# Three instead of two chunks of the memory queries with seven block products

## The chip, the cores and the metric

The kernel runs on one core of a Trainium2 chip. The metric is the device time of one launch in microseconds. TensorE (PE) multiplies; VectorE (DVE), ScalarE (ACT) and GpSimd (POOL) do the rest; SyncE (SP) issues the weight transfers.

## The reference

One decoder layer on 256 tokens of width 2048, in float32: a half-weighted SwiGLU, a mixer (gated spatial MLP beside windowed attention), cross-attention to 256 memory rows, a second half-weighted SwiGLU, and a last RMSNorm. The part around the change is the cross-attention:

```
q = (hn @ w_q).reshape(b, s, X_HEADS, X_HEAD_DIM)      # 256 x 2048 times 2048 x 2048, 4 heads of 512
kv = memn @ w_kv
scores = einsum('bshd,bmhd->bhsm', q, k) * X_HEAD_DIM ** -0.5
probs = softmax(scores)
out = einsum('bhsm,bmhd->bshd', probs, v).reshape(b, s, D_MODEL)
return out @ w_o
```

hn is RMSNorm(h) with the gain g_x, and h the residual stream.

## The kernel before, in words

**Products.** Every large matrix product is split in a high and a low part of fp32r (hi x hi, lo x hi, hi x lo), so each block product costs three matmuls of 128 x 128 weights against 512 columns. A product is cut into *units* of 1024 output columns (two blocks of 512), and a unit into 8 *chunks* of 256 rows of the weight. Over a chunk, a 2 x 2 block matrix of the activations (two token blocks, two row blocks) meets a 2 x 2 block matrix of the weights. `PRODUCTS` gives three ways to do that, one letter each: N, the plain 8 block products (24 matmuls); C, 8 block products arranged so that their sums share banks with S (24 matmuls); S, seven block products (21 matmuls). For S the activations need four more sums (`fill`, lines 219 to 238) and the weights four sums T1 to T4, which are then split in high and low parts as well (`load`, lines 328 to 359). Sums and splits are done by ScalarE (the high part, line 147) and VectorE (the low part, line 148; the sums, lines 337 to 341).

**Banks.** There are 8 PSUM banks in two pools of 4. A unit accumulates P2, Q3, Q4, Q5 in one pool (`acc`). The products that occur in S alone, P1, Q6 and Q7, take three banks of the other pool (`trp`) from the first S chunk of the unit on, until `seven_early` has read them behind the last S chunk. The pieces of side work use the same pool. `seven_late` combines the rest behind chunk 7.

**Buffers.** Raw weights have 3 buffers, their high and low parts 2 each, the sums T and their parts one each.

**Order on TensorE.** The order of TensorE is written by hand: chunk after chunk, and between them side work. `Unit.run` (line 425) calls `side_step` after every 6 matmuls; I call that a turn. A chunk of 24 matmuls has 4 turns, one of 21 has 3. Side work consists of generators; each step of one is a piece, and its `yield n` says after how many turns the next step may come. The core of it:

```
def side_step():
    now[0] += 1
    if ends[0] is not None and now[0] > ends[0]:
        return
    if not held[0] and not (tight[0] and now[0] < piece[0] + 3):
        for item in side:
            if item[0] <= now[0]:
                ...                    # one step of this item
                return
```

`tight` holds from the first S chunk of a `seven_unit` to its last: there pieces keep three turns apart. `have(pairs, i)` runs side work at once until the pair that a chunk needs exists. The order of the other engines is left to a planner, which follows the order of the program and when it takes an input to be ready.

**The stage of the change.** `KINDS_X` names the kinds of the 8 chunks of the two units `xq` (w_xq, lines 1371 to 1375); their activations are the pairs n3, made by `next_norm` (line 800) and shared by both units. Pairs 0 to 3 are made during the unit before, 4 to 7 in the first xq unit. Behind each xq unit `late_xq` puts two generators `attend_memory` (line 1296) on the list, one a head. Their steps: start (yield 1), transposes of the queries xqTp, twice (1, then 4), scores xs with softmax (5), transposes of the probabilities xpT (3), outputs xo, twice (1 each), and an empty last step. Heads 0 and 1 are attended during the second xq unit, heads 2 and 3 during the first unit of the output projection `xo` (w_xo). That is an `added_unit` (line 657) with the kinds NNNNNSNN: its S chunk takes all four `trp` banks, chunk 4 before it allows only two turns (`clear`), and chunk 5 asks for pair 7, so that all side work is done by then. Both heads' outputs are the pairs of this product, in order.

Other units: the memory keys and values (`mk`, `mv`) use `KINDS_M`, CCSCSCSC; the SwiGLU units use CCSCSCSC and SCSCSCSC.

Of the kernel before, what the change touches and what calls it, by code (L numbers as in the profile page):

```python
# [33 lines left out]
def layer_kernel(  # L34
# [528 lines left out]
    ORDER = ((0, 1, 2, 3, 4, 5, 6, 7), (0, 1, 3, 2, 4, 5, 6, 7))  # L563
    KINDS_M = "CCSCSCSC"
    KINDS_MIX = "CCCSCCSC"
    KINDS_X = "CCCSCSCC"

    KINDS_O = "NNNSNSNN"
    HALVES_O = ("NNNNNSNN", "NNNSNSNN")
# [21 lines left out]
    def seven_unit(s, kinds, w, cb, pairs, dst, late=None, beside=None, alone=(), order=range(8)):  # L591

        kinds = "".join(kinds[i] for i in order)
        u = Unit(s, kinds, alone=alone, sparse=True)
        got = {}

        def end():
            if dst is None:
                at = {(0, 0): got["p1"], (1, 1): s2(s), (0, 1): got["v"], (1, 0): got["z"]}
                seven_late(u, got, lambda tb, j: at[tb, j])  # L600
                late(at)
                return
            seven_late(u, got, dst)
            if late is not None:
                late()

        for i in range(8):
            push(
                u, i, w[order[i], cb], lambda i=i: have(pairs, order[i]),
                lambda i=i: (i == kinds.rindex("S") and seven_early(u, got), i == 7 and end()),  # L610
                beside=beside,
            )
# [674 lines left out]
    shared.clear()  # L1287
    n3, on3, rs3_ = next_norm("n3", G_X, KINDS_X)
    for cb in range(2):
# [74 lines left out]
    def late_xq(cb, at):  # L1364
        rs = rs3_()
        for j in range(2):
            for tb in range(TB):
                nc.scalar.activation(at[tb, j], at[tb, j], AF.Copy, scale=rs[:, tb:tb + 1])
            side_add(attend_memory(2 * cb + j, [at[tb, j] for tb in range(TB)]))

    for cb in range(2):
        seven_unit(
            "xq", KINDS_X, w_xq, cb, n3, None, lambda at, cb=cb: late_xq(cb, at),
            lambda i: rs3_() if i == 3 else None,
# [135 lines left out]
```

## Time and profile before

| | |
|---|---|
| median of 3 runs (lowest to highest) | 2034.7 us (2034.1 to 2034.9) |
| profiled execution, its own time | 2033.63 us |
| its span, 24271 instructions | 2031.9 us |
| TensorE busy | 2015.5 us (99%), granted clock 0.999 |
| TensorE weight loads | 1668.8 us (82%) |
| VectorE busy | 1853.6 us (91%) |
| ScalarE busy | 1313.2 us (65%) |
| first xq unit, from the span's start | 1135.06 to 1179.11 us |
| second xq unit | 1179.11 to 1235.98 us |

Times inside the profile are microseconds from the span's start. Matmuls overlap: the profile gives each some 0.39 us, while they follow each other every 0.227 us, so a busy TensorE is judged by the chain of waits, where each piece stands with the time that it adds. A row of a timeline has start, length, engine, line, operation, output and inputs, and in brackets how long the engine sat idle before it and what ended that.

### The profile page before, as it was taken

To read this page: it belongs to the slowest core of one execution; us is meant where nothing else is said; L and a number is where in the kernel's file an instruction comes from. 1 tells how busy PE (TensorE), PEld (TensorE's weight loads), DVE (VectorE), ACT (ScalarE), POOL (GpSimd) and SP (SyncE) were. 2 spreads that over 40 slices of the span, in tenths; PEclk is the share of its full clock that TensorE was granted. 3 is DMA by queue.
4 is the path that set the end of the run, shared out by engine and by line. 5 is a ranking of instruction groups with operands and counts; after the bars stand their busy time and mean duration, and the time that the engine had idled before them with its cause. 6 is when DMAs were issued, how large, how long until landed. Compare 5 with 4: busy or idle time off the path is not lost.

```text
span 2031.9 us, 24271 instructions
## 1 busy us (share of the span) xinstructions
PE 2015.5 (99%) x9203; PEld 1668.8 (82%) x9203; DVE 1853.6 (91%) x1994; ACT 1313.2 (65%) x1460; POOL 34.4 (2%) x57
## 2 busy tenths in 40 slices
PE   9999999999999999999999999999999999999998
PEld 7788888888888888888888888888888888888886
DVE  6999999999999978989879987899999999999998
ACT  7765566567665766755566666676656666676664
POOL 0000000000000010200000000000000000000000
PEclk9999999999999999999999999999999999999999
DMA  8666666666556575544675544556566656665563
GB/s 312 197 206 225 215 218 205 236 209 220 196 191 219 177 252 178 202 166 166 208 227 182 198 160 145 187 187 224 197 239 215 215 205 231 214 219 206 187 228 125
DMA packets 115333, 415.83 MB, mean 205 GB/s; under 512 B 61824, under 2 KB 63888, under 8 KB 68112
## 3 DMA queue, kind: packets, MB, share of 16 engines
q1 hardware_dynamic: 112768, 407.14, 57.6%
q0 software_dynamic: 2016, 6.30, 1.0%
q8 instruction: 72, 1.18, 0.2%
q10 hardware_dynamic: 432, 0.84, 0.1%
q14 instruction: 45, 0.37, 0.1%
HBM read 398.52 MB, written 2.10 MB: 197 GB/s over the span
## 4 chain that ended last, share of the span: by engine, by line
PE 85%; DVE 9%; issue 3%; ACT 2%; DMA 2%; SPq 0%; POOL 0%; POOLq 0%; DVEq 0%; ACTq 0%
PE f1gQ L428 12%; PE f2gQ L428 12%; PE f2dQ L428 6%; PE f1dQ L428 6%; PE f1gP L428 5%; PE f2gP L428 4%; PE xqQ L428 3%; PE f2dP L428 3%; PE f1dP L428 3%; PE woQ L428 2%; PE xoQ L428 2%; PE f2dR L428 2%; PE f1dR L428 2%; DVE f1gwl L148 2%; PE vQ L428 2%
## 5 line engine op out<-in xcount | busy, mean ns | idle before, releaser
L148 DVE TENSOR_TENSOR f1gwl<-f1gw,f1gwh 128x1536 fp32r<-128x1536 f32 (+2 forms) x94 | 181.6, 1934 | 24.5 <-ACT f1gwh L147 23.8
L147 ACT CAST f2gwh<-f2gw 128x1536 fp32r<-128x1536 f32 (+1 forms) x88 | 150.5, 1712 | 66.4 <-PE f2gQ L428 44.9
L148 DVE TENSOR_TENSOR f2gwl<-f2gw,f2gwh 128x1536 fp32r<-128x1536 f32 (+1 forms) x88 | 179.1, 2036 | 8.0 <-ACT f2gwh L147 8.0
L147 ACT CAST f1gwh<-f1gw 128x1536 fp32r<-128x1536 f32 (+2 forms) x94 | 153.1, 1629 | 45.0 <-PE f1gQ L428 19.3
L147 ACT CAST f1gth<-f1gt 128x1024 fp32r<-128x1024 f32 x76 | 79.9, 1051 | 103.1 <-DVE f1gt L337 68.7
L147 ACT CAST f2gth<-f2gt 128x1024 fp32r<-128x1024 f32 x82 | 85.4, 1050 | 64.2 <-DVE f2gt L341 34.0
L428 PE MATMUL f2gQ<-f2gwh,n4fh 128*128 128x512 f32 x317 | 123.8, 390 | 0.6 <-DVE f2gv L587 0.6
L428 PE MATMUL f2gQ<-f2gwh,n4fl 128*128 128x512 f32 x317 | 123.4, 389 | 0.0
L428 PE MATMUL f1gQ<-f1gwh,n1fl 128*128 128x512 f32 x286 | 111.4, 390 | 1.7 <-DVE n1fl L148 1.7
L428 PE MATMUL f1gQ<-f1gwh,n1fh 128*128 128x512 f32 x286 | 111.6, 390 | 0.0
L147 ACT CAST f2dwh<-f2dw 128x2048 fp32r<-128x2048 f32 (+1 forms) x44 | 77.4, 1758 | 47.5 <-PE f2dQ L428 39.5
L147 ACT CAST f1dwh<-f1dw 128x2048 fp32r<-128x2048 f32 (+1 forms) x44 | 77.3, 1757 | 43.7 <-PE f1dQ L428 42.7
L148 DVE TENSOR_TENSOR f1dwl<-f1dw,f1dwh 128x2048 fp32r<-128x2048 f32 (+1 forms) x44 | 92.0, 2092 | 12.0 <-ACT f1dwh L147 11.8
L148 DVE TENSOR_TENSOR f2dwl<-f2dw,f2dwh 128x2048 fp32r<-128x2048 f32 (+1 forms) x44 | 92.0, 2091 | 11.2 <-ACT f2dwh L147 11.1
L148 DVE TENSOR_TENSOR f2gtl<-f2gt,f2gth 128x1024 fp32r<-128x1024 f32 x82 | 99.5, 1218 | 1.0
L428 PE MATMUL f2gQ<-f2gwl,n4fh 128*128 128x512 f32 x317 | 96.7, 389 | 0.0
L148 DVE TENSOR_TENSOR f1gtl<-f1gt,f1gth 128x1024 fp32r<-128x1024 f32 x76 | 92.2, 1216 | 0.5
L428 PE MATMUL f1gQ<-f1gwl,n1fh 128*128 128x512 f32 x286 | 86.9, 389 | 0.0
L428 PEld LDWEIGHTS f2gQ<-f2gwh,n4fh 128*128 128x128 f32 x317 | 59.5, 188 | 13.8 <-DVE f2gv L587 1.6
L428 PEld LDWEIGHTS f2gQ<-f2gwh,n4fl 128*128 128x128 f32 x317 | 59.5, 188 | 12.2
L428 PEld LDWEIGHTS f2gQ<-f2gwl,n4fh 128*128 128x128 f32 x317 | 59.4, 188 | 12.3
L428 PE MATMUL f2gP<-f2gwh,n4fh 128*128 128x512 f32 x176 | 68.6, 390 | 0.0
(824 smaller groups left out, 6072.2 us busy)
## 6 DMA issues: line engine op xcount, KB each, us to landing
f2gw<-in_w_gu SPq DMA_DIRECT2D x88, 1024.0 KB, 4.9
f1gw<-in_w_gu SPq DMA_DIRECT2D x86, 1024.0 KB, 4.8
f1dw<-in_w_down SPq DMA_DIRECT2D x44, 1024.0 KB, 4.8
f2dw<-in_w_down SPq DMA_DIRECT2D x44, 1024.0 KB, 4.8
wow<-in_w_out SPq DMA_DIRECT2D x16, 1024.0 KB, 4.8
xqw<-in_w_xq SPq DMA_DIRECT2D x16, 1024.0 KB, 4.8
xow<-in_w_xo SPq DMA_DIRECT2D x16, 1024.0 KB, 4.8
qw<-in_w_in SPq DMA_DIRECT2D x8, 1024.0 KB, 4.8
```

The source lines that it names most:

```text
L147: nc.scalar.copy(hi, src)
L148: nc.vector.tensor_tensor(lo, src, hi.bitcast(F32), ALU.subtract)
L428: nc.tensor.matmul(self.banks[name], x, y, start=name not in self.begun, stop=self.left[name] == 0)
```

## The change

One string. The kinds of the 8 chunks of both xq units become CCSCSCSC: chunks 2, 4 and 6 are S, where 3 and 5 were. The pairs n3 follow (pairs 2, 4, 6 of kind S; the others of kind C), and so do the weights that `load` prepares, the span of `tight` (chunks 2 to 6 instead of 3 to 5), the place of `seven_early` (behind chunk 6 instead of 5) and the number of turns in a unit (29 instead of 30).

```diff
     ORDER = ((0, 1, 2, 3, 4, 5, 6, 7), (0, 1, 3, 2, 4, 5, 6, 7))
     KINDS_M = "CCSCSCSC"
     KINDS_MIX = "CCCSCCSC"
-    KINDS_X = "CCCSCSCC"
+    KINDS_X = "CCSCSCSC"
```

## The prediction

> **What bounds the kernel now.** I read the head of the page, then the chain of waits over the two units of memory queries and the output projection behind them, then busy times stage by stage.
>
> ```profile
> PE 2015.5 (99%) x9203; PEld 1668.8 (82%) x9203; DVE 1853.6 (91%) x1994; ACT 1313.2 (65%) x1460; POOL 34.4 (2%) x57
> ...
> 1135.06:1179.11 44.05, 44.05 (x203) 36.49 (x203) 37.09 (x43) 31.04 (x41) 1.12 (x1) 1.00 0.55 192
> 1179.11:1235.98 56.87, 56.86 (x307) 48.70 (x307) 44.80 (x54) 36.75 (x52) 0.00 (x0) 1.00 0.43 156
> ...
> 1441.00:1482.00 41.00, 41.00 (x183) 33.96 (x182) 40.42 (x38) 25.23 (x21) 0.00 (x0) 1.00 0.64 227
> ```
>
> Columns: stretch, length, then busy PE, PEld, DVE, ACT, POOL, clock, DMA share, GB/s. The first two stretches are the two xq units, the third lies in the second SwiGLU. TensorE is never idle in them, at full clock. VectorE has 7.0 us to spare in the first unit and 12.1 in the second; in the third it is busy 40.42 of 41.00 us and TensorE still loses nothing.
>
> ```profile
> 1153.27 1.36 PE xqP L428 x6
> ...
> 1158.03 0.91 PE xqP L428 x4
> ...
> 1163.47 1.36 PE xqP L428 x6
> ...
> 1190.74 2.86 PE xs L169 x24
> ...
> 1197.71 2.87 PE xs L169 x24
> ...
> 1203.33 0.44 PE xpT L1332 x4
> ```
>
> These are rows of the chain (start, length, what). A matmul costs 1.36/6 = 0.227 us. Chunk 3, of kind S, runs from 1153.27 to 1158.03 = 4.76 us (21 matmuls); chunk 4, of kind C, to 1163.47 = 5.44 us (24). What lies on the path here is TensorE's own program order, with the attention pieces (xs scores, xpT transposes, xo outputs) set between matmuls.
>
> **The change, part by part.**
>
> *TensorE.* Each unit gets S at chunks 2, 4, 6 instead of 3, 5: one more S, 3 matmuls fewer. Two units: 6 x 0.227 = **-1.36 us**, all on the path.
>
> *Weight splitting.* One more S load in each unit.
>
> ```profile
> L147 ACT CAST xqwh<-xqw x16: 1482/1906/1921, 1127.8 to 1218.8; 128x2048 fp32r<-128x2048 f32 x12, 128x1536 fp32r<-128x1536 f32 x4
> L148 DVE TENSOR_TENSOR xqwl<-xqw,xqwh x16: 1748/2284/2293, 1129.9 to 1220.7; 128x2048 fp32r<-128x2048 f32 x12, 128x1536 fp32r<-128x1536 f32 x4
> ...
> L337 DVE TENSOR_TENSOR xqt<-xqw x4: 1217/1222/1226, 1137.2 to 1199.3; 128x1024 f32<-128x1024 f32 x4
> L340 DVE TENSOR_TENSOR xqt<-xqt,xqw x4: 680/686/694, 1138.5 to 1200.5; 128x512 f32<-128x512 f32 x4
> L341 DVE TENSOR_TENSOR xqt<-xqt,xqw x4: 682/685/692, 1139.2 to 1203.5; 128x512 f32<-128x512 f32 x4
> ...
> L147 ACT CAST xqth<-xqt x8: 1037/1046/1070, 1139.5 to 1208.0; 128x1024 fp32r<-128x1024 f32 x8
> L148 DVE TENSOR_TENSOR xqtl<-xqt,xqth x8: 1212/1218/1226, 1142.0 to 1211.4; 128x1024 fp32r<-128x1024 f32 x8
> ```
>
> VectorE for S: 1.22 + 0.69 + 0.69 (sums) + 1.75 + 2 x 1.22 (splits) = 6.79 us; for C: 2.28. So +4.5 us a unit on VectorE, and 1.48 + 2 x 1.05 - 1.91 = +1.7 on ScalarE. Among the pairs of n3 made inside the first unit (4 to 7) there are two of kind S instead of one, under 1 us more. VectorE's first unit becomes 37.1 + 5.4 = 42.5 of 43.4 us, or 98%; the second 49.3 of 56.2. The third stretch above (99%, alternating C and S) shows TensorE fed at such a share, so I take **0**. Cover is VectorE's 7 us of idle time; gone, at most the excess over it would show: 0 to 2 us, from bunching early in the unit. The 16 loads of 1 MB on SP's queue keep size and order.
>
> *Where the attention pieces go.* This is counted in the code. After every 6 matmuls comes a turn (4 in C, 3 in S); a turn may issue one piece; from first to last S pieces keep 3 turns apart. Head 0 and head 1 of a unit's output are attended during the next 8 chunks. For the second xq unit before, the count puts the pieces of head 0 / head 1 at turns: transposes 2, 3 / 5, 6; xs 7 / 10; xpT 12 / 23; xo 15 and 18 / 26 and 27, which are the starts that the chain shows (xs at 1190.74 and 1197.71, xpT at 1203.33). After, with the spaced region from chunk 2 to 6: xs 7 / 10; xpT 13 / 25; xo 16 and 19 / 28 and 29 of 29. All twelve still fit, but an empty last step of head 1 falls into the next unit's first turn, and everything of heads 2 and 3 behind it (first output projection unit) comes one turn later. There chunks 0 to 3 give 16 turns and chunk 4 only two; at chunk 5 what is left is forced out at once, since S there needs all four PSUM banks.
>
> Three prices follow.
>
> (a) *Bank in chunk 2.* S takes three of the four side banks (P1, Q7, Q6) from its start to the end of chunk 6. Now head 1's xs comes 12 matmuls into that chunk, with only the bank that head 0's xs still holds. Before, S began a chunk later. The bank is free after the second exponential's sum:
>
> ```profile
> 1199.43 0.20 ACT L1320 ACTIVATION_READ_ACCUMULATOR pr<-xs,xmx 128x1 f32 x1
> ...
> 1204.43 0.20 ACT L1320 ACTIVATION_READ_ACCUMULATOR pr<-xs,xmx 128x1 f32 x1
> ...
> 1247.40 2.95 PE xs L169 x24
> ...
> 1253.37 0.20 ACT L1320 ACTIVATION_READ_ACCUMULATOR pr<-xs,xmx 128x1 f32 x1
> ```
>
> xs ends at 1193.60, 1200.58 and (chain: 1247.40 + 2.95) 1250.35: the release comes 6.0, 4.1 and 3.2 us later. The room is 18 matmuls = 4.1 us, so the stall is 0 to 1.9. Same place, same work: 6.0, less the 0.53 by which S's first split (1.75) is shorter than C's (2.28) in the queue ahead: **+1.4**. Behind it nothing runs on TensorE; VectorE gains time.
>
> (b) *Chunk 4 of the projection.* It needs head 2's first output.
>
> ```profile
> 1264.64 1.43 PE xo L169 x12
> ...
> 1267.46 1.43 PE xo L169 x12
> 1268.89 0.93 PE xoP L428 x4
> ...
> 1271.64 0.44 PE xpT L1332 x4
> ...
> 1274.85 2.87 PE xo L169 x24
> ...
> 1266.11 0.59 ACT L147 CAST xofh<-xo 128x512 fp32r<-128x512 f32 x1 [0.36 <-PE xo L169]
> ...
> 1266.73 0.69 DVE L148 TENSOR_TENSOR xofl<-xo,xofh 128x512 fp32r<-128x512 f32 x1 [0.51 <-ACT xofh L147]
> ```
>
> Now xo (1264.64) has 6 matmuls and the second xo before chunk 4 begins at 1268.89. One turn later it is the last thing ahead of chunk 4: its end to the low half is 1267.42 - 1266.07 = 1.35 us, and the chunk's second matmul reads that half. **+1.35**; ends 0.6 (high half alone) and 2.
>
> (c) *Head 3's transposes.* Now they run from 1271.64 to 1272.08, at the last allowed turn of chunk 4; after, that turn goes to head 2's closing step, and xpT is forced out with the two xo (the row of 24 at 1274.85) directly behind it.
>
> ```profile
> 1272.12 0.59 ACT L147 CAST xpTs<-xpT 128x512 fp32r<-128x512 f32 x1 [0.17 <-PE xpT L1332]
> ...
> 1272.74 0.69 DVE L148 TENSOR_TENSOR xpTs<-xpT,xpTs 128x512 fp32r<-128x512 f32 x1
> 1274.99 2.29 DVE L148 TENSOR_TENSOR xowl<-xow,xowh 128x2048 fp32r<-128x2048 f32 x1 [1.56 <-ACT xowh L147]
> 1277.19 0.68 DVE L148 TENSOR_TENSOR xofl<-xo,xofh 128x512 fp32r<-128x512 f32 x1
> ```
>
> At best the low half is there 1.34 us after the transposes (1272.08 to 1273.43). But issued at 1274.85 they would end at 1275.29 (0.44 long), while VectorE is in the 2.29 us split of chunk 6's weights and starts its next work at 1277.19; then 0.69: 1277.9. **+2.6**, ends 1.3 and 3.3 (head 0's own: 1203.77 to 1207.03).
>
> ```profile
> 1206.36 0.67 DVE L148 TENSOR_TENSOR xpTs<-xpT,xpTs 128x512 fp32r<-128x512 f32 x1
> ```
>
> Nothing on TensorE fills these waits, though chunk 5's weights are ready:
>
> ```profile
> 1315.72 0.50 PE L428 MATMUL xoQ<-xoth,xofh 128*128 128x512 f32 x1 [1.17 <-ACT n4r L266]
> ```
>
> Here one matmul waits 1.17 us for a bank, and the following ones wait with it. [...]
>
> The end of the units (P1 copied, the combinations in one chunk instead of two) I cost at nothing: VectorE's seven combinations a unit (the row below) take 4.8 us in all, against 5.4 us of chunk 7, and the memory key units already run the new order CCSCSCSC:
>
> ```profile
> L586 DVE TENSOR_TENSOR xq<-xqQ,xqz x2: 683/684/684, 1176.6 to 1233.4; 128x512 f32<-128x512 f32 x2
> ...
> 960.43:1002.85 42.42, 42.42 (x192) 35.24 (x192) 36.95 (x36) 21.30 (x19) 0.69 (x1) 1.00 0.54 198
> ```
>
> The last row's 183 matmuls are 41.5 us and one attention piece 0.8: no gap. Without cover, 0.5. Equally the 1.17 us wait above could go or double when ScalarE's order moves: 0, ends -1.2 and +1.2.
>
> **Sum**: -1.36 + 1.4 + 1.35 + 2.6 = +4.0 us. The profiled execution took 2033.63 (span 2031.9 and 1.7 around it), 1.1 below the median of the runs, 2034.7. By the median: **2038.7 us**.
>
> **Rivals.**
>
> 1. *Full gain.* Waits are hidden: the softmax clears its bank within 4.1 us (two of three rows do), and the order on ScalarE and VectorE is arranged so that the late pieces arrive in time. 2034.7 - 1.4 = 2033.3. Against it: the one-turn slip is certain by count, and (b) has no work between producer and consumer. [...]
>
> 2. *Small net loss.* Only (b) and the low end of (c): -1.36 + 1.35 + 1.3 = +1.3, so 2036.0. It decides if the low half of xpTs goes ahead of the weight split on VectorE.
>
> 3. *VectorE becomes the bound in the first unit.* At 98% a late S split of chunk 4 stalls TensorE. It decides when VectorE's backlog passes the spare 0.9 us: with 2 us of bunching and (a) to (c), +6.0, so 2040.7. Against: the SwiGLU row at 99%.
>
> **How the numbers follow.** The measurement tells 0.2% (4.07 us) from no change: 2030.6 to 2038.8. Forecast (+3 to +5) 0.45, rival 2 (0 to +3) 0.25, rival 1 (below 0) 0.12, rival 3 (above +5) 0.18. The forecast sits on the edge of the band: half of it, and rival 3, count as slower, 0.41; rivals 1 and 2 with the other half as same, 0.55; faster 0.04, for orders elsewhere that fall better. Range: from 2033.9, in rival 1, to 2041.9: the upper ends of (a), (b) and (c) give 2040.6, and 1.3 of the bunching comes to it. About 0.1 is left out on each side.
>
> **What would show it.** In the trace after: xqP and xqQ 3 matmuls fewer a unit; a wait of TensorE ahead of head 1's xs in chunk 2 of the second unit (a); a gap of about 1.3 us ahead of the projection's chunk 4 (b); xpT directly ahead of the row of 24 xo, with 1.3 to 2.6 us between (c). No gap at these places proves rival 1 right; gaps inside the first unit that end at VectorE's splits, rival 3. I would be wrong as well if the pieces do not slip by one turn, or if the later stages shift by themselves.

## The result, and the profile after

The changed kernel takes 2045.18 us in the median of 4 runs (2044.91 to 2049.38), the kernel before 2034.4 us (2032.45 to 2034.9): 1.0058 of the time before, 95% interval 1.0045 to 1.0071, so 10.8 us slower. The prediction was 2038.7 us with a range to 2041.9: the direction was right, the size was not.

The head of the page, and the two xq units, in the same cut as before (chunk 0 of the first unit to chunk 0 of the projection):

```profile
PE 2019.4 (99%) x9197; PEld 1671.9 (82%) x9197; DVE 1862.5 (91%) x2006; ACT 1316.6 (64%) x1464; POOL 33.9 (2%) x57
```

```profile
1134.58:1178.43 43.85, 43.68 (x200) 35.86 (x200) 40.87 (x50) 31.85 (x42) 0.69 (x1) 1.00 0.57 205
1178.43:1234.64 56.21, 56.14 (x304) 48.12 (x304) 45.62 (x53) 38.10 (x49) 0.00 (x0) 1.00 0.43 150
```

TensorE has 6 matmuls fewer (9197 for 9203) and is busy 3.9 us longer. The two units together take 100.06 us instead of 100.92: 0.86 us of the 1.36 arrive. The loss comes behind them. The list of TensorE's own waits (total, times, longest) begins before with these two, which the changed kernel has as well; from 1130 to 1293 us it has none:

```profile
PE f1gQ L428 <- DVE n1fl L148: 1.7, 1, 1.7
PE xoQ L428 <- ACT n4r L266: 1.2, 1, 1.2
```

After, it has these:

```profile
PE xoQ L428 <- DVE xqv L587: 2.9, 1, 2.9
PE xo L169 <- DVE xpTs L148: 2.1, 1, 2.1
...
PE xoP L428 <- DVE xofl L148: 1.1, 1, 1.1
PE xo L169 <- ACT xpTs L147: 0.8, 1, 0.8
PE xoP L428 <- ACT xofh L147: 0.7, 1, 0.7
...
PE xqP L428 <- DVE xqwl L148: 0.2, 1, 0.2
```

All but the last stand in the first unit of the output projection, in chunk 0 (xqv: line 587 still reads the bank that the matmul needs), ahead of chunk 4 (xofh, xofl: the high and low half of head 2's output) and around head 3's xo (xpTs: its transposed probabilities). Two of them are followed by something that no row of before has. The chain first (start, length, what), then busy times by stretch (granted clock third from the end), the last row from before:

```profile
1238.88 2.93 PE xoQ L428 x6
...
1283.51 5.28 PE xo L169 x23
1288.79 1.88 PE xoP L428 x6
```

```profile
1236.00:1238.00 2.00, 0.03 (x1) 0.00 (x0) 2.00 (x3) 0.28 (x1) 0.00 (x0) 1.00 0.00 0
1238.00:1240.00 2.00, 1.11 (x3) 0.93 (x4) 2.00 (x5) 1.26 (x2) 0.00 (x0) 0.63 0.79 233
1240.00:1242.00 2.00, 2.00 (x7) 1.57 (x5) 1.28 (x5) 1.61 (x4) 0.00 (x0) 0.52 0.72 299
...
1284.00:1286.00 2.00, 2.00 (x11) 2.00 (x11) 0.00 (x0) 0.00 (x0) 0.00 (x0) 0.50 0.66 266
1286.00:1288.00 2.00, 2.00 (x12) 2.00 (x11) 0.69 (x1) 0.59 (x1) 0.00 (x0) 0.50 0.52 217
```

```profile
1236.00:1293.00 57.00, 57.00 (x309) 49.01 (x308) 45.83 (x57) 37.45 (x56) 0.00 (x0) 1.00 0.39 137
```

Six matmuls take 2.93 us instead of 1.36, 23 xo take 5.28 instead of 2.75 (0.12 each): TensorE runs at about half clock (a granted clock of 0.50 to 0.52 where a row lies wholly behind a wait) behind each of the two long waits. The mean clock fell from 0.999 to 0.996.

The sum, from chunk 0 of the first xq unit to chunk 5 of the projection: before 1277.72 - 1135.06 = 142.66 us, after 1288.79 - 1134.58 = 154.21, +11.55. The terms: -1.36 (matmuls), +0.5 (chunk 4 of the first xq unit), +2.9 and +1.6 (chunk 0's wait, and the half clock behind it), +1.7 (ahead of chunk 4), +2.9 and +3.0 (head 3's xo, and the half clock on them and on the six matmuls behind). That is +11.2; 0.3 are spread.

Theory A for the experiments: the pieces come later, TensorE waits for them in order, and its clock halves behind the longer waits. Theory B: the third S chunk's work on VectorE makes everything late, wherever the pieces stand.

### The profile page after: what moved, and what is told of

It reads as the page before. It is cut to its first block, busy times and chain, and to the rows that moved or that the text cites. A ratio compares the mean times of both kernels' runs of the same rounds, so it can differ in the third digit from the quotient of the medians.

```text
span 2043.2 us, 24280 instructions
## 1 busy us (share of the span) xinstructions
PE 2019.4 (99%) x9197; PEld 1671.9 (82%) x9197; DVE 1862.5 (91%) x2006; ACT 1316.6 (64%) x1464; POOL 33.9 (2%) x57
## 4 chain that ended last, share of the span: by engine, by line
PE 88%; DVE 8%; issue 2%; ACT 1%; DMA 0%; POOL 0%; SPq 0%; POOLq 0%; DVEq 0%; ACTq 0%
PE f2gQ L428 15%; PE f1gQ L428 12%; PE f2dQ L428 6%; PE f1dQ L428 6%; PE f2gP L428 5%; PE f1gP L428 5%; PE f2dP L428 3%; PE f1dP L428 3%; PE woQ L428 2%; PE xoQ L428 2%; PE xqQ L428 2%; PE f2dR L428 2%; PE f1dR L428 2%; DVE f1gwl L148 2%; PE vQ L428 2%
```

## The experiments

**Only the spaced region as before (e_short).** Changed kernel, with

```diff
-            tight[0] = u.sparse and first <= i <= last
+            tight[0] = u.sparse and first <= i <= (min(last, 5) if u.s == "xq" else last)
```

> The changed kernel (kinds CCSCSCSC) with one edit: in the xq units the spaced region, in which pieces keep three turns apart, ends with chunk 5 as before, not with the last S chunk 6. By count the pieces of the second unit's head 1 are back at the turns of before (xpT 23, xo 26 and 27, empty step 28 of 29), and heads 2 and 3 start one turn earlier. Theory A (the time is lost because the pieces come later): the waits of TensorE of 3.0 us in chunk 0 of the projection, 1.7 us ahead of its chunk 4 and 2.9 us around head 3's xo go, and with them the stretches at half clock behind two of them; what is left is -1.36 for six matmuls and +0.6 for the wait ahead of chunk 4 of the first xq unit: 2033.6 us. Theory B (the third S chunk's 9 us more on VectorE make the combinations and splits late, wherever the pieces stand): that load is unchanged, 2043 to 2046 us.

Measured: 2034.08 us, ratio 1.0002 (0.9993 to 1.0011). All 11 us are gone, with all three S chunks and their loads in place: theory B falls. TensorE's waits in the same stretch that are new:

```profile
PE xs L169 <- DVE mkl L148: 0.4, 1, 0.4
PE xqTp L1304 <- ACT xqz L1368: 0.2, 1, 0.2
PE xqP L428 <- DVE xqwl L148: 0.2, 1, 0.2
```

The six matmuls still do not show. Measured from chunk 0 of the first xq unit, the forced pair of head 3's xo begins at 1273.76 - 1133.81 = 139.95 us; before, 1274.85 - 1135.06 = 139.79. So 1.36 us were saved and 1.5 lost: 0.5 in chunk 4 of the first unit and 1.0 in the first chunks of the projection, where the rows name 0.6.

**Only one empty turn, in the kernel before (e_slip).**

```diff
         rs = rs3_()
+        if cb == 1:
+            side_add(iter(()))
```

> The kernel before (kinds CCCSCSCC) with one edit: an empty item is put on the list ahead of heads 2 and 3, so that their pieces come one turn later. No engine gets more work. Theory A: the waits ahead of the projection's chunk 4 (1.7 us) and around head 3's xo (2.9 us) appear, and about 2.9 us from a halved clock behind the latter: +7.5, 2042 us; at least +4.6 if the clock holds. Theory B: no S chunk more, so no change: 2034.4 us.

Measured: 2040.89 us, ratio 1.0036 (1.0023 to 1.0050). Nothing was added but an empty turn, and it costs 6.9 us. TensorE's waits, and two rows of its timeline:

```profile
PE xo L169 <- DVE xpTs L148: 2.1, 1, 2.1
PE xo L169 <- ACT xpTs L147: 0.8, 1, 0.8
PE xoP L428 <- ACT xofh L147: 0.7, 1, 0.7
PE xoP L428 <- DVE xofl L148: 0.3, 1, 0.3
```

```profile
1274.98 0.60 PE L1332 MATMUL xpT<-ident,pr 128*128 128x128 f32 x4
...
1278.87 4.18 PE L169 MATMUL xo<-xpTs,mvh 128*128 128x256 f32 x23 [2.07 <-DVE xpTs L148]
```

xpT stands directly ahead of the xo that need it, head 3's waits are those of the changed kernel, and the xo are slow again (4.18 us). The wait ahead of chunk 4 is there too, but shorter: 1.0 us, where the changed kernel has 1.7.

**Only heads 2 and 3 back in time (e_tail).** Changed kernel, the empty step run off before the new heads are listed:

```diff
         rs = rs3_()
+        while side:
+            side_run(side[0])
```

> The changed kernel with one edit: what is left of head 1 (its empty last step) is run off before heads 2 and 3 are put on the list, so that these start at the turns of before. Head 1's last xo stays at the end of chunk 7. Theory A: the waits ahead of chunk 4 and around head 3's xo and the half clock behind the latter go (7.5 us), the wait of 3.0 us in chunk 0 and the 1.6 us of half clock behind it stay: 2038 us. If chunk 0's wait is only the first of a chain of lateness that the later ones follow from: 2045 us. Theory B: 2045 us.

Measured: 2037.78 us, ratio 1.0018 (1.0009 to 1.0028), 7.4 below the changed kernel. Of the three waits one is left, with its half clock (waits, then a stretch):

```profile
PE xoQ L428 <- DVE xqv L587: 2.9, 1, 2.9
```

```profile
1240.00:1242.00 2.00, 2.00 (x8) 1.62 (x7) 0.65 (x3) 0.33 (x1) 0.00 (x0) 0.50 0.49 197
```

So 7.4 us hang on the slip of heads 2 and 3, and chunk 0's wait does not bring the other two by itself.

**Only chunk 0's wait (e_c22).** Changed kernel; the block that line 586 writes no longer shares its 6 buffers with head 1's probabilities:

```diff
-                at = {(0, 0): got["p1"], (1, 1): s2(s), ...}
+                at = {(0, 0): got["p1"], (1, 1): m4(s)[:, :512], ...}
```

> The changed kernel with one edit: the fourth block that the xq unit's combinations write is taken from another pool of SBUF buffers, so that it needn't wait for a buffer that head 1's xpT holds until its last xo at the end of chunk 7. Pieces stay late. Theory A with the buffer as the cause of chunk 0's wait: VectorE does that combination right after the one ahead of it, chunk 0 doesn't wait, 3.0 us and 1.6 us of half clock go: 2040.6 us. If VectorE's load is the cause (theory B): 2045 us.

Measured: 2039.27 us, ratio 1.0024 (1.0014 to 1.0035), 5.9 below the changed kernel, and the wait on xqv is gone from TensorE's list, while those on xofh, xofl and xpTs are left, and the half clock behind the last (two of the waits, then a row of the chain):

```profile
PE xoP L428 <- ACT xofh L147: 0.7, 1, 0.7
PE xoP L428 <- DVE xofl L148: 0.2, 1, 0.2
```

```profile
1278.02 4.51 PE xo L169 x23
```

The two savings, 7.4 and 5.9, add to 13.3 us, more than the 12.1 of waits and half clock in the sum above (the 10.8 lost are net of the matmuls saved). Part of the loss hangs on both causes: without chunk 0's wait the one ahead of chunk 4 is 0.9 us and not 1.7. And the half clock behind the same wait differs (these 23 xo take 5.28, 4.18 and 4.51 us in three kernels). VectorE's rows in the changed kernel show what happened there:

```profile
1229.06 0.68 DVE L580 TENSOR_TENSOR xqz<-xqQ,xqv 128x512 f32<-128x512 f32 x1
1232.48 0.69 DVE L148 TENSOR_TENSOR xofl<-xo,xofh 128x512 fp32r<-128x512 f32 x1 [2.73 <-ACT xofh L147]
1235.00 2.29 DVE L148 TENSOR_TENSOR xowl<-xow,xowh 128x2048 fp32r<-128x2048 f32 x1 [1.83 <-ACT xowh L147]
1237.21 0.42 DVE L226 TENSOR_TENSOR xof<-xor 128x256 f32<-128x256 f32 x1
1237.55 0.68 DVE L586 TENSOR_TENSOR xq<-xqQ,xqz 128x512 f32<-128x512 f32 x1
1238.15 0.68 DVE L587 TENSOR_TENSOR xqv<-xqQ,xqv 128x512 f32<-128x512 f32 x1
```

The combination of line 586 comes 8.5 us behind the one ahead of it (line 580), after VectorE sat idle 2.73 and 1.83 us, and 2.9 us behind chunk 0's begin (1234.64); before, it began at 1233.4, ahead of chunk 0 (1235.98). Head 1's last xo, moved to the end of chunk 7, still reads buffers of the same set; so the planner puts 586 and 587 behind the split of the next weights, and chunk 0's second bank is free only then. With another buffer line 586 follows line 580 at once in VectorE's order (e_c22):

```profile
1228.94 0.68 DVE L580 TENSOR_TENSOR xqz<-xqQ,xqv 128x512 f32<-128x512 f32 x1
1229.72 0.69 DVE L586 TENSOR_TENSOR xq<-xqQ,xqz 128x512 f32<-128x512 f32 x1
```

**Filling the waits (e_warm).** Changed kernel, plus 11 and 12 matmuls whose results nobody reads, ahead of chunk 0's waiting matmul and behind head 3's xpT (the edit's main part; the places of the two calls are left out):

```diff
+    def fillers(n, x, y):
+        o = bank("fill")
+        for _ in range(n):
+            nc.tensor.matmul(o, x, y, start=True, stop=True)
```

> The changed kernel with matmuls added that compute nothing needed: 11 (2.5 us) behind the first six of the projection's chunk 0, and 12 (2.7 us) behind head 3's xpT, each into a bank that nobody reads. They stand where TensorE waits 3.0 and 2.9 us anyway. Theory A, with the halved clock as a price of the idle time itself: the waits shrink to about 0.5 us, no matmul runs at half clock, and the 1.6 and 2.9 us behind the waits go though 23 matmuls were added: 2040.7 us. Rival: the matmuls behind the waits are slow for another reason (their operands, a port, the transfers under way): 2045 us or a little more. In the profile: granted clock 1.00 from 1230 to 1295, and the 23 xo behind the wait at 0.12 us each instead of 0.23.

Measured: 2041.31 us, ratio 1.0035 (1.0021 to 1.0049). With 23 matmuls more the kernel is 3.9 us faster. Its timeline and two stretches:

```profile
1238.61 0.50 PE L437 MATMUL xoQ<-xowh,xofh 128*128 128x512 f32 x1 [0.36 <-DVE xqv L599]
...
1283.37 3.01 PE L169 MATMUL xo<-xpTs,mvh 128*128 128x256 f32 x23 [0.39 <-DVE xpTs L148]
```

```profile
1270.00:1272.00 2.00, 0.94 (x4) 0.73 (x4) 1.08 (x2) 0.00 (x0) 0.00 (x0) 0.95 0.74 221
1272.00:1274.00 2.00, 2.00 (x9) 1.76 (x8) 0.00 (x0) 0.00 (x0) 0.00 (x0) 0.50 0.72 303
```

The 23 xo take 3.01 us instead of 5.28, so it is the idle time that slows them, not their operands. The last two rows are a miss: behind the unfilled wait ahead of chunk 4 (1.7 us, in two parts) the clock now halves too, where in the changed kernel it had not. Expected was 1.00 throughout. This profile is of the slowest of the four executions (2042.84 us at a mean granted clock of 0.998; the others took 2040.79 to 2041.35 at 0.999), so the others may not have lost this.

**No empty step (e_noempty).** Changed kernel; a head ends with its last xo:

```diff
             xo[i] = p
-            yield 1
+            if half == 0:
+                yield 1
```

> The changed kernel with the empty last step of a head dropped and nothing else; the spaced region still ends with the last S chunk. By count head 1's pieces come at turns 22, 25 and 26 of 29 and nothing falls into the projection. Theory A: all three waits and the half clock go; left is the 0.54 us ahead of chunk 4 of the first xq unit: 2033.2 us. If the length of the spaced region itself costs (banks in chunk 6): 2035 us or more.

Measured: 2033.01 us, ratio 0.9994 (0.9985 to 1.0003). The length of the spaced region is harmless by itself; what counted were the turns.

**Several edits together.** All three are on the changed kernel with the spaced region of before. e_best0 drops the empty step and takes the other buffer as well; e_later instead makes pairs 6 and 7 of n3 later, by the edit below; e_best has all four edits.

```diff
-                    yield 4 if i % 2 == 0 and mixed else 1
+                    yield 10 if s == "n3" and i == 6 else 4 if i % 2 == 0 and mixed else 1
```

> The changed kernel with three edits: the spaced region ends with chunk 5, the empty last step of a head is dropped, and the fourth block of the combinations comes from the other pool. By count head 1's pieces then come at turns 22, 25 and 26, ahead of those of the kernel before. With the spaced region alone undone, 1.36 us of matmuls went and 1.5 us of waits came: 0.54 ahead of chunk 4 of the first xq unit and 1.0 in the first chunks of the projection. Theory A: the latter go, the former stays: 2033.2 us, 0.8 below the kernel before. Theory B: VectorE's load keeps both: 2034.1 us.

> The changed kernel with the spaced region ending with chunk 5, and the pairs 6 and 7 of n3 (needed by chunks 6 and 7) made in chunk 3 of the first xq unit instead of chunk 1, behind the weight split of chunk 4 in the order of the program. If VectorE's backlog of pairs is what makes chunk 4 wait in that unit (0.54 us): that wait goes and the time is 2033.5 us. If the split of chunk 4 is late by its own chain (buffers free late, ScalarE first): the wait stays and the time is 2034.1 us.

> All four edits on the changed kernel: spaced region to chunk 5, no empty step, the fourth block from the other pool, pairs 6 and 7 later. Theory A: the six matmuls saved show whole, 1.36 us below the kernel before: 2032.7 us. Theory B: 2034 us.

Measured: e_best0 2032.79 us (ratio 0.9993, 0.9984 to 1.0002), e_later 2033.36 (0.9993, 0.9984 to 1.0003), e_best 2032.81 (0.9995, 0.9986 to 1.0004). In e_later and e_best the wait on xqwl is gone, so VectorE's backlog of pairs made chunk 4 of the first unit wait. The row of the forced pair of xo in the chain, of e_best0 and of e_best:

```profile
1273.55 2.87 PE xo L169 x24
```

```profile
1273.85 2.87 PE xo L169 x24
```

From chunk 0 of the first xq unit (1134.61 and 1135.15) they begin at 138.94 and 138.70 us, against 139.79 before: 0.85 and 1.1 us of the 1.36 are kept. That these are really faster than the kernel before is not shown by the times: every interval reaches 1.0.

**Control (e_ctrl).** The kernel before with the empty step dropped and the other buffer.

> The kernel before (kinds CCCSCSCC) with the empty last step dropped and the fourth block of the combinations from the other pool: the control for these two edits. Nothing on TensorE waits at these places in the kernel before, so theory A expects no change, 2034.3 us, and the 0.8 to 1.4 us below it in the kernels with three S chunks are the six matmuls. If it comes out at 2033 us, the edits themselves and not the third S chunk brought that.

Measured: 2034.26 us, ratio 1.0000 (0.9991 to 1.0009). The edits alone bring nothing measurable to the time of the kernel with two S chunks. In its profile the forced pair of xo stands at

```profile
1273.65 2.87 PE xo L169 x24
```

which is 139.49 us behind chunk 0 of the first xq unit (1134.16), 0.3 sooner than before; so 0.3 of the 0.85 to 1.1 us above may come from the edits and not from the third S chunk.

## Why the prediction was wrong, step by step

The matmuls: right, 6 fewer. VectorE's load: right in total (1862.5 us for 1853.6), high for the first unit (40.87 of 43.85 us, 93% and not 98%), wrong that it costs nothing; chunk 4 takes 5.2 us instead of 4.76, the place that rival 3 named, at a quarter of its price.

The count of turns: right in every piece (xpT, xo and the forced group stand where it put them), and e_slip shows that the slip alone costs 6.9 us.

(a), the bank in chunk 2, priced at 1.4: measured 0. Head 0's softmax cleared its bank earlier than in the row I took:

```profile
1190.11 2.86 PE xs L169 x24
...
1197.08 2.87 PE xs L169 x24
```

```profile
1193.59 0.68 DVE L1315 TENSOR_REDUCE xmx<-xs 128x2 f32<-128x512 f32 x1
```

```profile
1196.41 0.20 ACT L1320 ACTIVATION_READ_ACCUMULATOR pr<-xs,xmx 128x1 f32 x1
```

These are the chain, VectorE's and ScalarE's rows in the changed kernel. The maximum begins 0.6 us after the scores end (1192.97), and the bank is released at 1196.61, 3.6 us after them and 0.5 us before the second xs. In the row that I took, two splits (1.22 and 1.28 us) stood ahead of the maximum on VectorE, and one (1.05) ahead of the exponentials on ScalarE.

(b) priced at 1.35: measured 1.7 (0.68 and 1.05). The slip alone (e_slip) costs 1.0 there; in the changed kernel one more weight split stands ahead of the low half on VectorE, and e_c22, without chunk 0's wait, has 0.9:

```profile
1270.93 1.22 DVE L148 TENSOR_TENSOR xotl<-xot,xoth 128x1024 fp32r<-128x1024 f32 x1
1272.07 0.68 DVE L148 TENSOR_TENSOR xofl<-xo,xofh 128x512 fp32r<-128x512 f32 x1
```

(c) priced at 2.6: measured 2.9 (0.85 and 2.07), by the mechanism named, the weight split on VectorE ahead of the low half. No later matmul ran ahead of the waiting ones in (b) and (c): TensorE's timeline shows the idle times of 0.68, 1.05, 0.85 and 2.07 us whole, each directly ahead of the matmul that waits.

Two steps failed. First, "The end of the units [...] I cost at nothing": it cost 2.9 us. I compared busy times (4.8 against 5.4 us) and looked at units that have no side work at their end; I did not follow the buffer that the fourth combination writes, which head 1's moved xo holds. e_c22 shows this. Second, each wait was priced at its own length. Behind the two waits near 3 us TensorE ran at half clock, 1.6 and 3.0 us more; e_warm shows that it is the idle time that does it. Without the half clock the sum would be 2034.4 + 11.2 - 4.6 = 2041.0, inside the range, but that would have been luck in part: (a) did not cost its 1.4, and the end of the units, at nothing, cost 2.9.

Rival 1, the full gain, was out of reach as the pieces stood; with them put back, 0.85 to 1.1 us of its 1.36 are there, 0.3 of them perhaps through the other edits, and all of it below what the times can tell.

## What to carry to other kernels

Where the order of an engine's work is set by counting steps, a change that shortens the main work moves all that is counted in it: count the new places, and for each moved piece list what it produces, who is directly behind it, and which buffers it still holds. Price a wait of TensorE with the clock behind it: here waits of 2.9 us cost 4.4 to 6 us. A gain of six matmuls needs every engine's lateness watched, since half a microsecond in two places takes it back.

## What the runs showed of the hardware

The kernel before has a single wait of 1.69 us in its first SwiGLU and one of 1.17 us in the projection. The clock is full behind the first and over the stretch that holds the second:

```profile
67.96 0.50 PE L428 MATMUL f1gQ<-f1gwh,n1fl 128*128 128x512 f32 x1 [1.69 <-DVE n1fl L148]
```

```profile
68.00:70.00 2.00, 2.00 (x11) 1.69 (x12) 2.00 (x6) 1.50 (x2) 0.00 (x0) 1.00 0.75 233
...
1293.00:1335.00 42.00, 40.83 (x188) 33.49 (x187) 37.91 (x47) 30.91 (x40) 2.20 (x3) 1.00 0.61 215
```

The first of these waits stands in the changed kernel too (1.68 us, ended at 67.49), and there as well the clock behind it is 1.00. Behind idle times of 2.9 us (one whole, one broken by a single matmul) TensorE ran at about half clock in the changed kernel (granted clock 0.52 and 0.50 in 2 us behind its two), in e_slip (0.57), in e_tail (0.50) and in e_c22 (0.55), for some 3 to 6 us; not always at once, for in e_slip, whose wait ended at 1278.87, the clock was 1.00 until 1280 and 0.57 in the 2 us behind that. Behind 1.7 us in two parts it stayed at 1.00 in the changed kernel and fell to 0.50 in the profile of e_warm. Executions of one kernel differ too: the ten of e_tail took 2035.65 to 2040.44 us, at mean granted clocks from 0.997 to 0.999. So the same wait can cost its length or more; what decides it is not shown.
